# Strassen's scheme on three of eight pairs of k tiles in six groups of columns

## The chip, the cores and the metric

One Trainium2 chip, one of its cores. A kernel is one program that runs on five engines: TensorE (PE: matmuls; PEld: its weight loads), VectorE (DVE), ScalarE (ACT), GpSimd (POOL) and SyncE (SP, which here only issues DMA transfers). Each engine works through its own instructions in order and waits on semaphores for the others. The metric is the device time of one execution in microseconds; the kernel before takes 978.75 us in the median of three runs (978.57 to 978.86).

## The reference

One residual layer on x of 256 tokens by 2048 channels, float32. All large work is products of these 256 rows with weights, each 2048 deep:

```
h    = rmsnorm(x) ;  proj = h @ w_in          # 2048 x 16400: q k v o z | gates | u z | g_a g_b
h_t  = mlstm(q, k, v, i, f)                   # 8 heads of 256
y_a  = sigmoid(o) * norm(h_t) * silu(z_a)     # 2048 wide
y_b  = (multiscale_pool(u) @ pool_w) * silu(z_b)   # 1024 wide
merged = sigmoid(g_a) * (y_a @ w_proj_mlstm) + sigmoid(g_b) * (y_b @ w_proj_pool)
out    = x + rmsnorm(merged @ w_out)
```

## The kernel before, in words

**Precision.** Every float32 product is made of three matmuls of type float32r: each operand is split into a high part (a cast) and a low part (the operand less its high part), and high·high, low·high and high·low are added in PSUM. `hi_lo` does the split: the cast on ScalarE (line 62), the subtraction on VectorE (line 63).

**Stages.** (1) The input projection for the pooling branch and the mLSTM, with the statistics of the norm, the mLSTM gates, convolutions, pooling and the mLSTM itself run as side work in between. (2) For each of four blocks j of 512 columns: the two gates g_a and g_b (`xtiles(12 + j)` and `xtiles(16 + j)`, 16 k tiles each), the pooling projection (8 k tiles of `wpp`), the mLSTM projection (16 k tiles of `wpm`), then the merge, which is transposed to `m_h`, `m_l`. (3) The output projection in four blocks of 512 columns; the last is ordered so that the rows end one half after the other.

**A token block.** `tok_block` (line 112) makes 512 columns for both halves t of the tokens, in two PSUM banks of the pool `acc` (4 banks; a second pool, `sm`, has the other 4). It goes through the weights in tiles of 128 x 2048 (1 MB). SP loads a tile into `raw` (3 buffers). Each half of a tile, here called a **piece**, is split into `wh`, `wl` (128 x 1024 each, 4 buffers of each) and then used for 12 matmuls of 128x512: 8 with `wh` (high and low part of the activations), 4 with `wl`. A `raw` buffer is free for the next load when VectorE has made the low part of its second piece; a buffer of `wh` or `wl` is free when TensorE is through with the piece four before.

**Order.** The engines' orders come from a scheduler of the framework, which moves instructions forward where their operands allow. Side work is written as generators: `step()` after each piece lets each advance to its next `yield`. The statistics of the norm are such a generator (`stats`, line 231): four squares on ScalarE, a power on GpSimd that gives `rstd`, then `stats_bc` (line 256), which scales the identity by `rstd` on VectorE (`dg`, line 261) and spreads it over partitions by two small matmuls (line 262) into `rstd_bc`. The gates' matmuls (line 286) and ScalarE's sigmoid with `rstd` (line 573) belong to the same time.

Of the kernel before, what the change touches and what calls it, by code (L numbers as in the profile page):

```python
# [17 lines left out]
P = 128  # L18
D = 2048
# [7 lines left out]
WARM = 9  # L27
QD = 32
XW = T + 512
EPS = 1e-6  # L30
# [9 lines left out]
def block_kernel(ctx: ExitStack, tc: tile.TileContext, a: dict, out: bass.AP):  # L40
# [44 lines left out]

    xs_ctx = ExitStack()
    xp = xs_ctx.enter_context(tc.tile_pool(name="xp", bufs=1))
    xc = xp.tile([P, KT, 2, T], F32R, name="xc")
    ybp = xs_ctx.enter_context(tc.tile_pool(name="ybp", bufs=1))
    yb_h = ybp.tile([P, KT // 2, T], F32R, name="yb_h")  # L90
# [19 lines left out]

    def tok_block(tiles, st_h, st_l, load=w_tile):

        ps = [acc.tile([P, 512], F32, name="acc") for _ in range(2)]
        n = 4 * len(tiles)
# [117 lines left out]
    def stats():  # L232
# [17 lines left out]
        rsqrt_mean(rstd, ms, D)  # L250
        for _ in range(3):
            yield 1
        stats_bc()
        ready.append(1)

    def stats_bc():

        pb = small()
        for t in range(2):
            dg = sp.tile([P, P], F32, name="dg", bufs=2)  # L260
            nc.vector.tensor_scalar(dg, ident, rstd[:, t : t + 1], None, op0=ALU.mult)
            nc.tensor.matmul(pb[:, t * P : (t + 1) * P], ones_f, dg, start=True, stop=True)
        nc.vector.tensor_copy(rstd_bc, pb[:, :T])
# [177 lines left out]

    yp = xs_ctx.enter_context(tc.tile_pool(name="yp", bufs=1))
    y_h = yp.tile([P, KT, T], F32R, name="y_h")
# [155 lines left out]
    def st(tile_):  # L599
        return lambda k, t: tile_[:, k, t * P : (t + 1) * P]  # L600

    def merge(j, t, m):
        pt = small()
# [5 lines left out]
    def merges(j, ms):  # L609
        for t in range(2):  # L610
            yield 1
            merge(j, t, ms[t])

    for j in range(4):
        gs = []
        for n in range(2):
            pg = tok_block(xtiles(12 + 4 * n + j), xh, xl)
            for t in range(2):
                s = gate.tile([P, 512], F32, name="g", tag=f"g{t}")
                nc.scalar.activation(s, pg[t], AF.Sigmoid, scale=rstd[:, t : t + 1])  # L620
                gs.append(s)
        drain()
        if j == 0:
            ph1_ctx.close()
            late = ctx.enter_context(tc.tile_pool(name="late", bufs=1, side="right"))
            m_h = late.tile([P, KT, T], F32R, name="m_h")
            m_l = late.tile([P, KT, T], F32R, name="m_l")
        pb = tok_block(
            [a["wpp"][j, i].rearrange("p k c -> p (k c)") for i in range(2)], st(yb_h), st(yb_l)
        )  # L630
        for t in range(2):
            nc.vector.tensor_tensor(gs[2 + t], pb[t], gs[2 + t], op=ALU.mult)
        pa = tok_block(
            [a["wpm"][j, i].rearrange("p k c -> p (k c)") for i in range(4)], st(y_h), st(y_l)
        )
        for t in range(2):
            m = gs[t]
            nc.vector.tensor_tensor(m, pa[t], m, op=ALU.mult)
            nc.vector.tensor_tensor(m, m, gs[2 + t], op=ALU.add)
        side.append(merges(j, gs[:2]))  # L640
    xs_ctx.close()


    osplit = ctx.enter_context(tc.tile_pool(name="osplit", bufs=4, side="right"))
    fin = ctx.enter_context(tc.tile_pool(name="fin", bufs=1))
    post = fin.tile([P, D], F32, name="post")
    nc.scalar.dma_start(post, a["post"])
    xr = [fin.tile([P, D], F32, name=f"xr{t}") for t in range(2)]
    for t in range(2):
        nc.scalar.dma_start(xr[t], a["x"][t * P : (t + 1) * P, :])  # L650
    ob = [fin.tile([P, D], F32, name=f"ob{t}") for t in range(2)]
    s4 = fin.tile([P, 2, 5], F32, name="s4")
# [30 lines left out]

    def otiles(j):
        return [a["wo"][j, i].rearrange("p k c -> p (k c)") for i in range(4)]

    for j in range(3):
        po = tok_block(otiles(j), st(m_h), st(m_l), lambda src: w_tile(src, osplit))
        for t in range(2):
            sums(t, j, j * 512, (j + 1) * 512, po[t])  # L690
            weigh(t, j * 512, (j + 1) * 512, po[t])

    m_hi, m_lo = st(m_h), st(m_l)
    ws = []
    for half in range(8):
        if half % 2 == 0:
            raw = rawp.tile([P, 2048], F32, name="raw")
            nc.sync.dma_start(raw, otiles(3)[half // 2])
        pool, bufs = (fin, 4) if half < 4 else (osplit, None)
        wh = pool.tile([P, 1024], F32R, name="wh", bufs=bufs)  # L700
# [3 lines left out]
    for t, parts in ((0, 1), (1, 2)):  # L704
        for part in range(parts):
            n = 512 // parts
            po = acc.tile([P, 512], F32, name="acc")[:, :n]
            for k in range(KT):
# [17 lines left out]
def _tiles(w, cols, kk):  # L726

    k, n = w.shape
    r = w.reshape(k // (P * kk), kk, P, n // cols, cols)
    return np.ascontiguousarray(r.transpose(3, 0, 2, 1, 4))  # L730


# [57 lines left out]
```

## Time and profile before

| | |
|---|---|
| median of three runs | 978.75 us |
| the profiled execution | 978.46 us |
| its span | 976.7 us (so 1.8 us lie around it) |
| busy in the span: PE, PEld, DVE, ACT, POOL | 99%, 84%, 65%, 51%, 1% |
| TensorE clock granted | 0.998 of full |
| DMA | 187.74 MB, 192 GB/s in the mean |

The first gates' sigmoids start at 596 us, the first squares of the output at 903 us. Matmuls are pipelined and their ends are modelled: each is shown as 0.39 us long, though a next one starts every 0.23 us. So how much TensorE does is read from starts, and whether it waits from the list of waits.

### The profile page before, as it was taken

The page shows a single profiled execution, that of the slowest core. Times are in us where ns is not written, and L with a number is a line of the kernel's source. Part 1 is how long each engine was busy: PE and PEld are TensorE (multiplying, and loading weights), DVE is VectorE, ACT ScalarE, POOL GpSimd, SP SyncE. Part 2 cuts the span into 40 slices and gives each one's busy share as a digit, 9 for nine tenths or more (in the row PEclk, how much of TensorE's full clock was granted, in tenths as well). Part 3 has the DMA queues.
Part 4 walks back from the last instruction along what each step waited for, and adds up shares of the span by engine and source line. Part 5 has one row for each costly group of instructions (what it writes and reads, how often), then busy time and mean ns, then how long its engine had stood idle before and what let it go on. Part 6 is the DMA issues. An engine that isn't in the chain of part 4 may idle for free.

```text
span 976.7 us, 12410 instructions
## 1 busy us (share of the span) xinstructions
PE 965.9 (99%) x4785; PEld 816.4 (84%) x4785; DVE 630.6 (65%) x938; ACT 495.1 (51%) x678; POOL 14.5 (1%) x35
## 2 busy tenths in 40 slices
PE   9999999999999999999999999999999999999996
PEld 6888888888888888888888888888888888888886
DVE  7699776677766867758677686554454455455563
ACT  7756444456644665546554475444444434443451
POOL 1000000000000000000000000000000000000001
PEclk9999999999999999999999999999999999999999
DMA  9755445544455435564555544555555555567542
GB/s 355 296 187 209 173 173 177 211 172 172 157 197 207 173 134 211 172 216 136 191 191 192 196 172 168 179 207 179 178 195 193 210 172 199 189 248 268 180 167 86
DMA packets 29306, 187.74 MB, mean 192 GB/s; under 512 B 3264, under 2 KB 3648, under 8 KB 8256
## 3 DMA queue, kind: packets, MB, share of 16 engines
q1 hardware_dynamic: 28816, 183.81, 52.6%
q10 hardware_dynamic: 432, 3.15, 0.8%
q8 instruction: 37, 0.61, 0.2%
q14 instruction: 21, 0.17, 0.0%
HBM read 184.85 MB, written 2.10 MB: 191 GB/s over the span
## 4 chain that ended last, share of the span: by engine, by line
PE 60%; issue 38%; ACT 1%; POOL 0%; DMA 0%; DVE 0%; DVEq 0%; SPq 0%; POOLq 0%
PE acc L143 18%; PE acc L123 10%; PE acc L124 10%; PE acc L126 10%; PE acc L145 9%; PE sm L72 1%; PE sm L71 1%; PE sm L73 1%; ACT xw L245 0%; PE sm L286 0%; DMA xw<-in_xw 0%; PE sm L559 0%; DVE xr L677 0%; PE sm L508 0%; POOL xr L675 0%
## 5 line engine op out<-in xcount | busy, mean ns | idle before, releaser
L63 DVE TENSOR_TENSOR wl<-raw,wh 128x1024 fp32r<-128x1024 f32 x328 | 398.5, 1223 | 263.6 <-ACT wh L62 263.4
L62 ACT CAST wh<-raw 128x1024 fp32r<-128x1024 f32 x328 | 342.3, 1050 | 370.4 <-PE acc L124 251.9
L123 PE MATMUL acc<-wh,xc 128*128 128x512 f32 x640 | 251.2, 392 | 0.1
L124 PE MATMUL acc<-wh,xc 128*128 128x512 f32 x640 | 249.6, 390 | 0.0
L143 PE MATMUL acc<-xc,wh 128*128 128x512 f32 x768 | 192.5, 392 | 0.0
L126 PE MATMUL acc<-wl,xc 128*128 128x512 f32 x640 | 172.5, 389 | 0.0
L143 PEld LDWEIGHTS acc<-xc,wh 128*128 128x128 f32 x768 | 138.9, 189 | 25.6
L126 PEld LDWEIGHTS acc<-wl,xc 128*128 128x128 f32 x640 | 120.2, 188 | 25.2
L123 PEld LDWEIGHTS acc<-wh,xc 128*128 128x128 f32 x640 | 120.4, 188 | 24.7 <-ACT wh L62 1.0
L124 PEld LDWEIGHTS acc<-wh,xc 128*128 128x128 f32 x640 | 120.4, 188 | 23.9
L145 PEld LDWEIGHTS acc<-xc,wl 128*128 128x128 f32 x768 | 104.8, 190 | 7.5
L145 PE MATMUL acc<-xc,wl 128*128 128x256 f32 x768 | 107.1, 282 | 0.0
L123 PE MATMUL acc<-wh,y_h 128*128 128x512 f32 x128 | 49.8, 389 | 0.0
L124 PE MATMUL acc<-wh,y_l 128*128 128x512 f32 x128 | 49.8, 389 | 0.0
L473 DVE SCALAR_TENSOR_TENSOR cy<-pad,vec,cy 128x256 f32<-128x256 f32 x96 | 39.3, 477 | 0.0
L123 PE MATMUL acc<-wh,m_h 128*128 128x512 f32 x96 | 37.6, 391 | 0.0
L124 PE MATMUL acc<-wh,m_l 128*128 128x512 f32 x96 | 37.4, 389 | 0.0
L126 PE MATMUL acc<-wl,y_h 128*128 128x512 f32 x128 | 34.2, 389 | 0.0
L123 PEld LDWEIGHTS acc<-wh,y_h 128*128 128x128 f32 x128 | 24.0, 188 | 5.0
L124 PEld LDWEIGHTS acc<-wh,y_l 128*128 128x128 f32 x128 | 24.0, 188 | 5.0
L126 PEld LDWEIGHTS acc<-wl,y_h 128*128 128x128 f32 x128 | 24.0, 188 | 5.0
L126 PE MATMUL acc<-wl,m_h 128*128 128x512 f32 x96 | 25.7, 389 | 0.0
(197 smaller groups left out, 771.6 us busy)
## 6 DMA issues: line engine op xcount, KB each, us to landing
raw<-in_wx SPq DMA_DIRECT2D x76, 1024.0 KB, 4.7
raw<-in_wq SPq DMA_DIRECT2D x44, 1024.0 KB, 4.8
raw<-in_wpm SPq DMA_DIRECT2D x16, 1024.0 KB, 4.7
raw<-in_wo SPq DMA_DIRECT2D x16, 1024.0 KB, 4.9
raw<-in_wpp SPq DMA_DIRECT2D x8, 1024.0 KB, 4.7
xw<-in_xw SPq DMA_DIRECT2D x15, 384.0 KB, 6.0
raw<-in_wq SPq DMA_DIRECT2D x8, 512.0 KB, 8.1
xw<-in_x SPq DMA_DIRECT2D x4, 512.0 KB, 8.3
```

Of the source, the lines that this page charges most:

```text
L62: nc.scalar.copy(hi, src)
L63: nc.vector.tensor_tensor(lo, src, hi.bitcast(F32), op=ALU.subtract)
L71: nc.tensor.matmul(ps, lh, rh, start=start, stop=False)
L72: nc.tensor.matmul(ps, ll, rh, start=False, stop=False)
L73: nc.tensor.matmul(ps, lh, rl, start=False, stop=stop)
L123: nc.tensor.matmul(ps[t], st_h(k, t), wh[:, cols], start=k == 0, stop=False)
L124: nc.tensor.matmul(ps[t], st_l(k, t), wh[:, cols], start=False, stop=False)
L126: nc.tensor.matmul(ps[t], st_h(k, t), wl[:, cols], start=False, stop=k == n - 1)
L143: nc.tensor.matmul(ps[c], wh[:, cols], xc[:, k], start=k == 0, stop=False)
L145: nc.tensor.matmul(ps[c][:, 1], wl[:, cols], xc[:, k, 0], start=False, stop=k == KT - 1)
L473: nc.vector.scalar_tensor_tensor(y, pad[:, 1 + j : 1 + j + T], cw[:, j : j + 1], y, op0=ALU.mult, op1=ALU.add)
```

## The change

Six groups of 1024 columns are taken out of the token blocks: three of gates (g_b of blocks 0 and 1, g_a of 2 and 3, g_b of 2 and 3), two of the mLSTM projection, one of the output (columns 0 to 1023). A group has four results C (t, c), one for each half of the tokens and each half of the columns, in four banks. Its 16 k tiles are eight pairs (k, k + 8), and a load of 1 MB (`ws`) brings one pair for both halves of the columns. Five pairs go as before: two pieces of 12 matmuls. Three pairs (`NS`, numbers 0 to 2) go by Strassen's scheme in Winograd's form: seven products of blocks in place of eight, 21 matmuls in place of 24. The order of the pairs in a group is 3, 4, 0, 5, 1, 6, 2, 7.

- For the weights of such a pair VectorE makes four sums of blocks (`t13`, 128x1024; `t24`, two of 128x512), and the pair is split in four pieces of 512, 1024, 1024 and 1024 columns, with 3, 6, 6 and 6 matmuls.
- For the activations four sums are made once for each of x, y and m (`s_forms`), which takes two of the three `raw` buffers while it lasts.
- Four products add into four banks of the other PSUM pool, the rest straight into C; after the third pair these four are combined (`e11` to `e22`: two copies on ScalarE, four sums on VectorE), and added to C at the group's end.
- All gates come ahead of the projections now, and their results are kept; m takes the place of x in `xc`; output block 2 comes first, then the group of blocks 0 and 1, then block 3.
- In `stats` two `yield`s fewer come before `stats_bc`, and the first of its two matmuls is kept in program order.

```diff
@@ stats, stats_bc @@
         rsqrt_mean(rstd, ms, D)
-        for _ in range(3):
-            yield 1
+        yield 1
         stats_bc()
...
-            nc.tensor.matmul(pb[:, t * P : (t + 1) * P], ones_f, dg, start=True, stop=True)
+            i = nc.tensor.matmul(pb[:, t * P : (t + 1) * P], ones_f, dg, start=True, stop=True)
+            if t == 0:
+                tc.keep_in_program_order(i)
@@ new functions @@
+    def s_forms(hl):
+        f = rawp.tile([P, 2048], F32, name="raw")[:, : 2 * NS * T].rearrange("p (h k t) -> p h k t", h=2, k=NS)
+        for h in range(2):
+            nc.vector.tensor_tensor(f[:, h], hl(0, h).bitcast(F32), hl(1, h).bitcast(F32), op=ALU.add)
+        (a11, a21), (a12, a22) = ([f[:, h, :, t * P : (t + 1) * P] for t in range(2)] for h in range(2))
+        r = rawp.tile([P, 2048], F32, name="raw")[:, : 4 * NS * P].rearrange("p (s k t) -> p s k t", s=4, k=NS)
+        nc.vector.tensor_tensor(r[:, 0], a21, a22, op=ALU.add)
+        nc.vector.tensor_tensor(r[:, 1], r[:, 0], a11, op=ALU.subtract)
+        nc.vector.tensor_tensor(r[:, 2], a11, a21, op=ALU.subtract)
+        nc.vector.tensor_tensor(r[:, 3], a12, r[:, 1], op=ALU.subtract)
...
+        hi_lo(s_h, s_l, r)
+        return s_h, s_l
+
+    def group(gi, st_h, st_l, forms, get_a, get_b):
+        s_h, s_l = forms
+        C = {(t, c): get_a() for t in range(2) for c in range(2)}
...
+        for kp in order:
+            raw = rawp.tile([P, 2048], F32, name="raw")
+            nc.sync.dma_start(raw, a["ws"][gi, kp])
+            b4 = raw.rearrange("p (b n) -> p b n", b=4)
+            if kp >= NS:
+                for h in range(2):
...
+                    hi_lo(wh, wl, raw[:, h * 1024 : (h + 1) * 1024])
...
+                continue
...
+            nc.vector.tensor_tensor(t13, b4[:, 1:4:2], b4[:, 0:2], op=ALU.subtract)
+            nc.vector.tensor_tensor(t24[:, 0], b4[:, 3], t13[:, 0], op=ALU.subtract)
+            nc.vector.tensor_tensor(t24[:, 1], b4[:, 2], t24[:, 0], op=ALU.subtract)
...
+            for src, n, jobs in (
+                (raw[:, 0:512], 512, ((0, ps[0], x_(0, 0), last),)),
+                (raw[:, 1024:2048], 1024, (((0, 0), C[0, 0], x_(1, 0), False), ((0, 1), C[0, 1], form(3), False))),
+                (flat[0], 1024, ((1, ps[1], form(0), last), (3, ps[3], form(2), last))),
+                (flat[1], 1024, ((2, ps[2], form(1), last), ((1, 0), C[1, 0], x_(1, 1), False))),
+            ):
...
+                hi_lo(wh[:, :n], wl[:, :n], src)
...
+            if last:
...
+                nc.scalar.copy(e11, ps[0])
+                nc.scalar.copy(e22, ps[1])
+                nc.vector.tensor_tensor(e21, ps[2], e11, op=ALU.add)
+                nc.vector.tensor_tensor(e12, e21, e22, op=ALU.add)
+                nc.vector.tensor_tensor(e21, ps[3], e21, op=ALU.add)
+                nc.vector.tensor_tensor(e22, e21, e22, op=ALU.add)
+        return C, {(0, 0): e11, (0, 1): e12, (1, 0): e21, (1, 1): e22}
@@ gates, projections, output @@
-    for j in range(4):
-        gs = []
-        for n in range(2):
-            pg = tok_block(xtiles(12 + 4 * n + j), xh, xl)
...
+    for j in range(2):
+        pg = tok_block(xtiles(12 + j), xh, xl)
...
+    forms = s_forms(lambda part, h: xc[:, 8 * h : 8 * h + NS, part])
+    for gi, (n, j0) in enumerate(((1, 0), (0, 2), (1, 2))):
+        C, E = group(gi, xh, xl, forms, *((bank, small) if gi % 2 == 0 else (small, bank)))
+        for (t, c), ps in C.items():
+            g_ = lateg.tile([P, 512], F32, name=f"g{n}{j0 + c}{t}")
+            nc.vector.tensor_tensor(g_, ps, E[t, c], op=ALU.add)
+            nc.scalar.activation(g_, g_, AF.Sigmoid, scale=rstd[:, t : t + 1])
...
+    forms = s_forms(lambda part, h: (y_h, y_l)[part][:, 8 * h : 8 * h + NS])
...
+        C, E = group(3 + jp, st(y_h), st(y_l), forms, bank, small)
...
+    po2 = tok_block(otiles(2), st(m_h), st(m_l), get=small)
+    drain()
+    forms = s_forms(lambda part, h: (m_h, m_l)[part][:, 8 * h : 8 * h + NS])
...
+    C, E = group(5, st(m_h), st(m_l), forms, bank, small)
```

The scheduler's order shows the places at which instructions move. First TensorE in the statistics, behind the second piece of the first channel block. `acc_370`, `acc_371` are that block's banks, `wh_440` its third piece; `dg` carries `rstd`, `gc` are the gates' weights. Before:

```order
L145 MATMUL acc_370<-xc_76,wl_414 128x256
L145 MATMUL acc_371<-xc_76,wl_414 128x256
L262 MATMUL sm_589<-dg_590,ones_f_109 128x128
L262 MATMUL sm_589<-dg_593,ones_f_109 128x128
L286 MATMUL sm_663<-xc_76,gc0_405 128x512 x4
L286 MATMUL sm_663<-xc_76,gc1_407 128x512
L143 MATMUL acc_370<-xc_76,wh_440 128x512
L143 MATMUL acc_371<-xc_76,wh_440 128x512
```

With the change (lines of the new kernel) the third piece follows at once,

```order
L149 MATMUL acc_370<-xc_76,wl_414 128x256
L149 MATMUL acc_371<-xc_76,wl_414 128x256
L147 MATMUL acc_370<-xc_76,wh_440 128x512
L147 MATMUL acc_371<-xc_76,wh_440 128x512
L147 MATMUL acc_370<-xc_76,wh_440 128x512
```

and four pieces later (`wh_559` is the second block's third piece):

```order
L149 MATMUL acc_493<-xc_76,wl_523 128x256
L265 MATMUL sm_542<-dg_543,ones_f_109 128x128
L265 MATMUL sm_542<-dg_546,ones_f_109 128x128
L147 MATMUL acc_492<-xc_76,wh_559 128x512
L147 MATMUL acc_493<-xc_76,wh_559 128x512
```

The two matmuls with `dg` have moved back by four pieces, and the five of the gates that stood with them to where the other eleven are.

Second, VectorE around the first group. Before, it splits piece after piece, with the low parts of y in between (`wl_5555` is the last piece of the second gate block, `wl_5585` the first of the next block):

```order
L63 TENSOR_TENSOR wl_5487<-raw_5468,wh_5486 128x1024
L63 TENSOR_TENSOR wl_5505<-raw_5502,wh_5504 128x1024
L66 SCALAR_TENSOR_TENSOR y_l_1366<-sm_5434,vec_82,y_h_1365 128x256
L63 TENSOR_TENSOR wl_5521<-raw_5502,wh_5520 128x1024
L66 SCALAR_TENSOR_TENSOR y_l_1366<-sm_5434,vec_82,y_h_1365 128x256
L66 SCALAR_TENSOR_TENSOR y_l_1366<-sm_5459,vec_82,y_h_1365 128x256
L63 TENSOR_TENSOR wl_5539<-raw_5536,wh_5538 128x1024
L66 SCALAR_TENSOR_TENSOR y_l_1366<-sm_5459,vec_82,y_h_1365 128x256
L63 TENSOR_TENSOR wl_5555<-raw_5536,wh_5554 128x1024
L63 TENSOR_TENSOR wl_5585<-raw_5582,wh_5584 128x1024
```

With the change the six instructions of the forms (lines 612 to 618) stand between `wl_5487` and `wl_5555`, and in the group itself, from the first Strassen pair (`raw_5665`) over an ordinary one (`raw_5713`) to the second Strassen pair (`raw_5747`), VectorE has:

```order
L64 TENSOR_TENSOR wl_5684<-raw_5665,wh_5683 128x1024
L673 TENSOR_TENSOR t13_5749<-raw_5747 128x1024
L674 TENSOR_TENSOR t24_5750<-raw_5747,t13_5749 128x512
L64 TENSOR_TENSOR wl_5694<-t13_5671,wh_5693 128x1024
L675 TENSOR_TENSOR t24_5750<-raw_5747,t24_5750 128x512
L64 TENSOR_TENSOR wl_5704<-t24_5672,wh_5703 128x1024
L64 TENSOR_TENSOR wl_5716<-raw_5713,wh_5715 128x1024
L64 TENSOR_TENSOR wl_5732<-raw_5713,wh_5731 128x1024
L64 TENSOR_TENSOR wl_5755<-raw_5747,wh_5754 128x512
L64 TENSOR_TENSOR wl_5762<-raw_5747,wh_5761 128x1024
L64 TENSOR_TENSOR wl_5772<-t13_5749,wh_5771 128x1024
L673 TENSOR_TENSOR t13_5827<-raw_5825 128x1024
```

The sums of the second Strassen pair stand ahead of the last two pieces of the first one; those of the third (`t13_5827`) behind the second's third piece.

Third, VectorE at the end of the third gate group, where the forms of y (`raw_6589`, `raw_6592`) are made; `wl_6514`, `wl_6524` are the last two pieces of its last Strassen pair, `raw_6543` is its last pair, `wl_6607` the first piece of the pooling projection:

```order
L612 TENSOR_TENSOR raw_6589<-y_h_1365,y_l_1366 128x768
L64 TENSOR_TENSOR wl_6514<-t13_6491,wh_6513 128x1024
L615 TENSOR_TENSOR raw_6592<-raw_6589 128x384
L617 TENSOR_TENSOR raw_6592<-raw_6589 128x384
L616 TENSOR_TENSOR raw_6592<-raw_6592,raw_6589 128x384
L64 TENSOR_TENSOR wl_6524<-t24_6492,wh_6523 128x1024
L64 TENSOR_TENSOR wl_6546<-raw_6543,wh_6545 128x1024
L618 TENSOR_TENSOR raw_6592<-raw_6589,raw_6592 128x384
L64 TENSOR_TENSOR wl_6562<-raw_6543,wh_6561 128x1024
L698 TENSOR_TENSOR e2_6535<-sm_6333,e0_6533 128x512
```

Since the forms hold two `raw` buffers, the pooling projection's first load takes that of `raw_6543`, which `wl_6562` frees.

More of the change, by code (lines that the diff above doesn't have):

```diff
@@ L109, in w_tile, with bank, tok_block @@
             yield c0, c1, wh, wl
-    def tok_block(tiles, st_h, st_l, load=w_tile):
-        ps = [acc.tile([P, 512], F32, name="acc") for _ in range(2)]
+    def bank():
+        return acc.tile([P, 512], F32, name="acc")
+    def tok_block(tiles, st_h, st_l, load=w_tile, get=bank):
+        ps = [get() for _ in range(2)]
         n = 4 * len(tiles)
@@ L602, in merge @@
     def merge(j, t, m):
-        pt = small()
+        pt = bank()
         for c in range(4):
@@ L620, in block_kernel @@
-                nc.scalar.activation(s, pg[t], AF.Sigmoid, scale=rstd[:, t : t + 1])
-                gs.append(s)
+                nc.vector.tensor_tensor(gs[1, j, t], pb[t], gs[1, j, t], op=ALU.mult)
         drain()
[L623 to L630, printed above, removed]
```

136 lines of the change are left out of this document (103 added, 33 removed).

## The prediction

> **What bounds the kernel now.** The page's busy shares, then TensorE's list of waits, then rows by stage:
>
> ```profile
> PE 965.9 (99%) x4785; PEld 816.4 (84%) x4785; DVE 630.6 (65%) x938; ACT 495.1 (51%) x678; POOL 14.5 (1%) x35
> PE sm L262 <- DVE dg L261: 1.6, 1, 1.6
> PE sm L166 <- DVE zeros L161: 1.2, 1, 1.2
> 700.00:750.00 50.00, 50.00 (x226) 41.38 (x225) 26.81 (x27) 21.24 (x22) 0.00 (x0) 1.00 0.53 190
> ```
>
> A PE busy share of 99% alone would prove little, since matmuls are shown longer than their spacing. The waits do: in the whole span TensorE waits for another engine twice, both at the start. In the stage of gates and projections (the last row: stretch, sum, PE, PEld, DVE, ACT, POOL, clock, DMA share, GB/s) VectorE has 26.8 of 50 us, ScalarE 21.2, DMA half its time. So a matmul taken out there counts in full, until another engine becomes late. What one costs is read from VectorE's beat in a token block, where each low part waits for a buffer that TensorE gives back:
>
> ```profile
> 908.45 1.22 DVE L63 TENSOR_TENSOR wl<-raw,wh 128x1024 fp32r<-128x1024 f32 x1 [1.50 <-ACT wh L62]
> 911.17 1.23 DVE L63 TENSOR_TENSOR wl<-raw,wh 128x1024 fp32r<-128x1024 f32 x1 [1.50 <-ACT wh L62]
> 913.89 1.23 DVE L63 TENSOR_TENSOR wl<-raw,wh 128x1024 fp32r<-128x1024 f32 x1 [1.50 <-ACT wh L62]
> ```
>
> One piece, 12 matmuls, every 2.72 us: 0.227 us a matmul.
>
> **The change part by part. Matmuls.** Each group drops 3 of 24 in three pairs: 6 x 3 x 3 = 54, so 54 x 0.227 = **-12.2 us**. The 1 MB loads stay as many. A group lasts (5 x 24 + 3 x 21) x 0.227 = 41.5 us on TensorE; a Strassen pair 4.8 us, an ordinary one 5.4.
>
> **VectorE in a group.** Its prices:
>
> ```profile
> L63 DVE TENSOR_TENSOR wl<-raw,wh 128x1024 fp32r<-128x1024 f32 x328 | 398.5, 1223 | 263.6 <-ACT wh L62 263.4
> L639 DVE TENSOR_TENSOR g<-g 128x512 f32<-128x512 f32 x8 | 5.1, 682 | 0.0
> L632 DVE TENSOR_TENSOR g<-acc,g 128x512 f32<-128x512 f32 x8 | 5.2, 686 | 4.4 <-PE acc L126 4.4
> 931.85 3.50 DVE L63 TENSOR_TENSOR wl<-raw,wh 128x1024 fp32r<-128x1024 f32 x3 [0.42 <-ACT wh L62]
> 904.15 1.28 DVE L660 TENSOR_TENSOR ob<-acc,post 128x512 f32<-128x512 f32 x2
> ```
>
> Three in a row take 3.50 us where one takes 1.22, so they start (3.50 - 1.22) / 2 = 1.14 us apart; two of 512 take 1.28, 0.60 apart, or 0.72 where one needs the other's result (0.68 and a hand-over of 0.04). Between the two sizes lie 1.05 ns an element; by that line 768 elements take 0.95 us (0.87 apart), 384 take 0.55, 1536 take 1.76: estimates. A group has 19 low parts of 1024 (21.7 us), 3 of 512 (1.8), 3 `t13` (3.4), 6 halves of `t24` (4.0), 4 sums of e (2.6) and 4 additions to C (2.4): 35.9 of 41.5 us, 87%, in place of 16 low parts, 18.2. In the stretch of one Strassen and one ordinary pair it is 9.2 (6.9 without the lead that the two next sums may take, and 2.3) of 10.2. It is not the bound, but near it, and it keeps TensorE covered only while it is some pieces ahead. Four buffers of `wl` let it be three pieces ahead, 8 us in ordinary pieces, 4 in Strassen's. ScalarE has 10 casts of 1.05, three of 0.61, nine more of 1.05, two copies and four sigmoids, about 26 us: covered.
>
> **Entry to the first group.** The last gate block before, with the times of its last pieces (VectorE's order is in the section on the change):
>
> ```profile
> 596.13 1.21 DVE L63 TENSOR_TENSOR wl<-raw,wh 128x1024 fp32r<-128x1024 f32 x1
> 602.06 0.19 PEld L123 LDWEIGHTS acc<-wh,xc 128*128 128x128 f32 x1
> 604.35 1.05 ACT L62 CAST wh<-raw 128x1024 fp32r<-128x1024 f32 x1 [1.31 <-PE acc L124]
> 605.44 1.23 DVE L63 TENSOR_TENSOR wl<-raw,wh 128x1024 fp32r<-128x1024 f32 x1 [1.11 <-ACT wh L62]
> 606.70 16.59 SPq L104 DMA_DIRECT2D raw<-in_wpm  x4
> raw<-in_wx SPq DMA_DIRECT2D x76, 1024.0 KB, 4.7
> GB/s 0 0 0 0 0 170 210 380 433 393 92 66 144 301 419 433 315 26 0 0 105 262 433 419 419 39 0 0 52 170 223 406 446 380 0 0 0 210 39 393
> L620 ACT ACTIVATE g<-acc,rstd 128x512 f32<-128x512 f32 x16 | 10.1, 684 | 0.0
> ```
>
> The cast at 604.35 is that of the block's last piece, and waited for the piece four before, which TensorE began at 602.06; so the block ends at 602.06 + 5 x 2.72 = 615.7. The forms put 2 x 0.87 and about 2.2 us of sums ahead of the low part at 605.44; idle time takes up part, and it ends at 607.4, not 606.7. Then the freed buffer is loaded, landing 4.7 us later at 612.2; the next load, issued with it, 2.4 us behind (1 MB at 433 GB/s, the highest of 40 slices around it) at 614.6. Four casts, the last after 614.6 + 1.05 + 0.95 = 616.6, stand ahead of the two sigmoids that empty the banks of the block, and the group's third and fourth bank are those two. TensorE asks for the third at 615.7 + 4 x 0.227 = 616.6 and gets it at 617.3: **+0.7 us** (nothing if the second load lands 0.7 us sooner; 1.6 with VectorE 1 us later).
>
> **Forms of y.** The pooling projection's first load waits for `wl_6562`. From there: landing 4.7, cast 1.05, hand-overs 0.2: 6.0 us. `wl_6562` cannot be made before TensorE is through with the piece four before; then TensorE still has 1.36 + 1.36 + 2.72 + 2.72 = 8.2 us and VectorE's 1.2 go off, 6.9 left: no wait. If VectorE is late by all it does for the forms up to there (1.7 + 2.2 = 4.0 us), 2.9 are left: 3.1 us of wait. From `wl_6497` on VectorE has 10.0 us for these six pieces with the forms, TensorE 10.2: it neither gains nor loses, and I take it 1.9 us behind its best: **+1.0**. The forms of m follow ordinary pieces, with 10.9 us in place of 8.2 behind the freeing low part: nothing.
>
> **Loads within a group.** The second and third Strassen pair's loads wait for the second low part of an ordinary pair; between that and their first sum VectorE has 4.2 and 2.9 us of work, the landing takes 4.7. So VectorE idles 0.5 and 1.8, 2.3 us a group: 35.9 + 2.3 = 38.2 is still below 41.5, and its lead hides it. With the merges' additions and the last block's start I allow **+1.2** in all, between nothing and 6 x 2.3 = 13.8.
>
> **Statistics.** TensorE, ScalarE:
>
> ```profile
> 32.10 1.11 PE L145 MATMUL acc<-xc,wl 128*128 128x256 f32 x8
> 34.84 0.71 PE L262 MATMUL sm<-dg,ones_f 128*128 128x128 f32 x4 [1.63 <-DVE dg L261]
> 35.31 1.41 PE L286 MATMUL sm<-xc,gc 128*128 128x512 f32 x5
> 36.55 2.00 PE L143 MATMUL acc<-xc,wh 128*128 128x512 f32 x8
> 34.50 0.72 ACT L573 ACTIVATE g<-g,rstd 128x512 f32<-128x512 f32 x1 [1.21 <-POOL rstd L193]
> 35.13 1.04 ACT L62 CAST wh<-raw 128x1024 fp32r<-128x1024 f32 x1
> ```
>
> The wait for `dg` goes, but the piece that comes up in its place has its cast at 35.13, behind a sigmoid that waits for the same `rstd`. TensorE then waits until 36.2: the piece starts 0.3 us earlier than at 36.55, and the 1.7 us of work from 34.84 to 36.55 that filled this time is done later. Less about 0.2 for two matmuls without a wait: **+1.2 us**. What is late next is `rstd_bc`, at 47.7 in place of 35.6; the side work behind it feeds no piece.
>
> The sum: -12.2 + 0.7 + 1.0 + 1.2 + 1.2 = -8.1 against the profiled execution's 978.46 gives 970.4; the median shown is 0.3 higher, so I say **970.5 us**.
>
> [...] By row 931.85 an instruction of VectorE starts 0.09 us before the one ahead ends. [...]
>
> **The rivals.** (1) *VectorE's lead covers everything*: only matmuls and statistics count, 978.46 - 12.2 + 1.2 + 0.3 = 967.7. For it: 87%. Against: the two entries above are worked out from landings, not shares. Chance 0.12.
>
> (2) *VectorE loses its lead at every form and seam*: each of three forms costs the 3.1 us of the worst case, the entry 1.6, and half of the load waits, 6.9, go through: -12.2 + 1.2 + 1.6 + 9.3 + 6.9 = +6.8 at the worst, 985.5; with half of these stalls -12.2 + 1.2 + 8.9 = -2.1, 976.6. I put it at 975 to 978. For it: a VectorE a few per cent slower than its rows (strided operands, which no row shows) would do it. Against: the sizes are those of rows. Chance 0.14.
>
> (3) *VectorE's instructions take their full length each*: 42 of them a group in the mean, 0.085 more each, 3.6 us; with forms 3.0 us a group, 35.9 + 3.6 + 3.0 = 42.5 against 41.5. It is the bound: six times 1.0 us. An engine that is behind anyway cannot lose a lead again, so I count the three forms' 3.1 and the entry's 1.6 by half, 5.5: -12.2 + 1.2 + 6.0 + 5.5 = +0.5, 979.3, no change. Chance 0.04.
>
> (4) *Slower: the loads of the Strassen pairs.* The 2.3 us that VectorE idles for two loads in each group reach TensorE, since the sums stand ahead of the last pieces of the pair before: 6 x 2.3 = 13.8 more in place of 1.2, 978.46 - 12.2 + 1.2 + 0.7 + 1.0 + 13.8 + 0.3 = 983.3. It decides where VectorE stands less than 2.3 us ahead of TensorE when it comes to `t13`. For it: three `raw` buffers and the order of the sums. Against: its lead of three pieces. Chance 0.09.
>
> That fewer matmuls are dropped than said is excluded by the order's count.
>
> **How the numbers follow.** 0.2%, 2 us, is about what a measurement of this kernel can tell from no change, so faster ends at 976.8 and slower begins at 980.7. Forecast 0.61 (967 to 974), the rivals as given: faster is 0.61 + 0.12 + two thirds of (2) = 0.82; same 0.05 of (2) and 0.04 of (3), 0.09; slower 0.09. The range goes from 966.5, 1.2 below rival (1), to the end of (2), 977.5; outside lie (3), (4) and a little.
>
> **What would show it.** TensorE's wait for `dg` gone and one of 3 us for a cast at 33 to 36 us in its place; one of under 1.6 us for a sigmoid at the first group's third bank; one of 0 to 3 us for a cast at the pooling projection's first piece; VectorE some 87% busy in the groups, with waits for `raw` ahead of `t13`. Wrong would be: repeated waits of TensorE for low parts inside groups (2, 4), or a beat of VectorE of 1.22 us in a row of three (3).

## The result and the profile after

The changed kernel takes 971.25 us in the median of four runs (970.8 to 971.56), the kernel before beside it 978.66 us. The ratio is 0.9924 with a 95% interval of 0.9911 to 0.9936: 7.4 us faster. The forecast was 970.5 us, with a range of 966.5 to 977.5.

The profiled execution took 971.45 us, with a span of 969.6. From its page, the busy shares:

```profile
PE 956.9 (99%) x4731; PEld 807.4 (83%) x4731; DVE 746.3 (77%) x1097; ACT 535.5 (55%) x730; POOL 14.5 (1%) x35
```

TensorE's list of waits in the whole span (us in total, times, the longest):

```profile
PE acc L147 <- ACT wh L63: 3.0, 1, 3.0
...
PE acc L641 <- ACT g L721: 0.6, 1, 0.6
```

TensorE has 54 matmuls fewer (4785 to 4731), VectorE 116 us more work. Two waits are new, both announced: 3.0 us for a cast, and 0.6 us for a sigmoid at the first group's third bank. None stands in the groups, and none at the pooling projection. The span fell by 976.7 - 969.6 = 7.1 us, 5.1 less than the 12.2 of the matmuls alone. Where these 5.1 us are is read at three places.

**The statistics.** TensorE's timeline from the second piece of the first channel block on (start, duration, engine, line):

```profile
31.96 1.11 PE L149 MATMUL acc<-xc,wl 128*128 128x256 f32 x8
36.07 3.69 PE L147 MATMUL acc<-xc,wh 128*128 128x512 f32 x8 [3.00 <-ACT wh L63]
40.55 2.00 PE L147 MATMUL acc<-xc,wh 128*128 128x512 f32 x8
```

The same time in stretches of 1 us; the third number from the end is the granted clock:

```profile
36.00:37.00 1.00, 0.93 (x2) 0.81 (x3) 0.95 (x1) 1.00 (x3) 0.00 (x0) 0.56 0.04 16
37.00:38.00 1.00, 1.00 (x4) 0.75 (x3) 0.67 (x2) 1.00 (x2) 0.00 (x0) 0.50 0.00 0
38.00:39.00 1.00, 1.00 (x4) 0.81 (x3) 1.00 (x2) 1.00 (x2) 0.00 (x0) 0.50 0.00 0
39.00:40.00 1.00, 1.00 (x6) 0.85 (x6) 1.00 (x2) 0.68 (x2) 0.00 (x0) 0.73 0.54 66
```

The piece that comes up in place of the `dg` matmuls waits until 36.07, as forecast (36.2). But then its eight matmuls show 3.69 us where before, at 36.55, they showed 2.00: the granted clock is 0.50. The rows add up to 0.88 + 1 + 1 + 0.54 = 3.4 us at half clock. The piece after it, in the timeline of before:

```profile
39.34 2.00 PE L143 MATMUL acc<-xc,wh 128*128 128x512 f32 x8
```

Now it starts 40.55 - 31.96 = 8.59 us behind the second one; before, it was 39.34 - 32.10 = 7.24, and 1.7 us of that was other work, which is now done later (some 0.2 us shorter, without its wait). So 1.35 + 1.7 - 0.2 = 2.85 us, in place of the 1.2 forecast.

**The entry to the first group.** TensorE there:

```profile
619.39 0.39 PE L643 MATMUL acc<-wh,xc 128*128 128x512 f32 x1
620.35 0.50 PE L641 MATMUL acc<-wh,xc 128*128 128x512 f32 x1 [0.57 <-ACT g L721]
```

The first row is the fourth matmul, the last on the first two banks; then comes the third bank. It would have started at 619.39 + 0.23 = 619.62 and starts at 620.35, 0.73 later; the matmul behind it loses another 0.1.

**Inside the groups.** The stretch of the three gate groups (stretch, sum, PE, PEld, DVE, ACT), and that of the first group of the mLSTM projection:

```profile
618.71:744.92 126.21, 125.64 (x551) 102.99 (x550) 110.15 (x119) 74.12 (x83) 0.00 (x0) 1.00 0.52 191
766.68:808.46 41.78, 41.78 (x185) 34.36 (x184) 33.66 (x35) 22.63 (x25) 0.00 (x0) 1.00 0.55 194
```

TensorE in a Strassen pair (six matmuls from the first row to the last), and in an ordinary pair (four):

```profile
653.12 0.40 PE L641 MATMUL sm<-wh,s_h 128*128 128x512 f32 x1
...
654.52 0.40 PE L641 MATMUL sm<-wh,s_h 128*128 128x512 f32 x1
...
656.60 0.39 PE L643 MATMUL acc<-wh,xc 128*128 128x512 f32 x1
...
657.50 0.39 PE L643 MATMUL acc<-wh,xc 128*128 128x512 f32 x1
```

VectorE is busy 110.15 of 126.21 us, 87%, as worked out. A group without a stall lasts 41.78 us where 183 matmuls at 0.2267 make 41.48. The 0.3 us are no wait: in the Strassen pair the starts lie (654.52 - 653.12) / 6 = 0.233 us apart, in the ordinary one (657.50 - 656.60) / 4 = 0.225. Six groups make 1.8 us.

So -12.2 + 2.85 + 0.83 + 1.8 = -6.7, which leaves 0.4 of the measured -7.1 to small differences elsewhere.

### The profile page after: what moved, and what is told of

It is laid out like the page before. It is cut to its first block, busy times and chain, and to the rows that moved or that the text cites. A ratio compares the mean times of both kernels' runs of the same rounds, so it can differ in the third digit from the quotient of the medians.

```text
span 969.6 us, 12590 instructions
## 1 busy us (share of the span) xinstructions
PE 956.9 (99%) x4731; PEld 807.4 (83%) x4731; DVE 746.3 (77%) x1097; ACT 535.5 (55%) x730; POOL 14.5 (1%) x35
## 4 chain that ended last, share of the span: by engine, by line
PE 61%; issue 37%; ACT 1%; POOL 0%; DVE 0%; DVEq 0%; ACTq 0%; POOLq 0%
PE acc L147 18%; PE acc L127 10%; PE acc L128 10%; PE acc L130 10%; PE acc L149 9%; PE sm L72 1%; PE sm L73 1%; PE sm L74 1%; PE sm L170 0%; PE sm L291 0%; ACT xw L249 0%; PE sm L564 0%; DVE xr L799 0%; PE sm L513 0%; POOL xr L797 0%
## 5 line engine op out<-in xcount | busy, mean ns | idle before, releaser
L64 DVE TENSOR_TENSOR wl<-raw,wh 128x1024 fp32r<-128x1024 f32 (+1 forms) x328 | 387.0, 1191 | 140.6 <-ACT wh L63 138.5
L63 ACT CAST wh<-raw 128x1024 fp32r<-128x1024 f32 (+1 forms) x328 | 334.7, 1028 | 281.8 <-PE acc L147 96.0
L127 PE MATMUL acc<-wh,xc 128*128 128x512 f32 x448 | 175.8, 392 | 0.0
L128 PE MATMUL acc<-wh,xc 128*128 128x512 f32 x448 | 174.7, 390 | 0.0
L130 PE MATMUL acc<-wl,xc 128*128 128x512 f32 x448 | 121.2, 389 | 0.0
L130 PEld LDWEIGHTS acc<-wl,xc 128*128 128x128 f32 x448 | 84.1, 188 | 17.7
L127 PEld LDWEIGHTS acc<-wh,xc 128*128 128x128 f32 x448 | 84.2, 188 | 17.5 <-ACT wh L63 1.2
L128 PEld LDWEIGHTS acc<-wh,xc 128*128 128x128 f32 x448 | 84.2, 188 | 16.5
L63 ACT CAST wh<-t 128x1024 fp32r<-128x1024 f32 x36 | 37.9, 1052 | 53.5 <-PE acc L643 41.4
L64 DVE TENSOR_TENSOR wl<-t,wh 128x1024 fp32r<-128x1024 f32 x36 | 44.0, 1223 | 20.1 <-ACT wh L63 20.1
L641 PE MATMUL acc<-wh,xc 128*128 128x512 f32 x141 | 55.0, 390 | 0.6 <-ACT g L721 0.6
L643 PE MATMUL acc<-wh,xc 128*128 128x512 f32 x141 | 55.0, 390 | 0.0
L645 PE MATMUL acc<-wl,xc 128*128 128x512 f32 x141 | 40.5, 390 | 0.0
L643 PE MATMUL acc<-wh,y_l 128*128 128x512 f32 x92 | 35.9, 390 | 0.0
L641 PE MATMUL acc<-wh,y_h 128*128 128x512 f32 x92 | 35.8, 390 | 0.0
L641 PEld LDWEIGHTS acc<-wh,xc 128*128 128x128 f32 x141 | 26.5, 188 | 6.6 <-ACT g L721 1.0
L645 PEld LDWEIGHTS acc<-wl,xc 128*128 128x128 f32 x141 | 26.5, 188 | 5.6
```

Source lines behind the costliest of these rows:

```text
L63: nc.scalar.copy(hi, src)
L64: nc.vector.tensor_tensor(lo, src, hi.bitcast(F32), op=ALU.subtract)
L127: nc.tensor.matmul(ps[t], st_h(k, t), wh[:, cols], start=k == 0, stop=False)
L128: nc.tensor.matmul(ps[t], st_l(k, t), wh[:, cols], start=False, stop=False)
L130: nc.tensor.matmul(ps[t], st_h(k, t), wl[:, cols], start=False, stop=k == n - 1)
L641: nc.tensor.matmul(dst, lh, wh, start=key not in begun, stop=False)
```

## The experiments

The theories at the start: **A**, the costs lie where the changed trace shows them, 2.8 us in the statistics (half of it clock), 0.8 at the third bank, and a Strassen pair is worth its matmuls. **B**, the prediction's own sizes, 1.2 us for the statistics. Behind them stood the question how far VectorE was from being the bound.

### The statistics as before

```diff
-        yield 1
+        for _ in range(3):
+            yield 1
         stats_bc()
...
-            i = nc.tensor.matmul(pb[:, t * P : (t + 1) * P], ones_f, dg, start=True, stop=True)
-            if t == 0:
-                tc.keep_in_program_order(i)
+            nc.tensor.matmul(pb[:, t * P : (t + 1) * P], ones_f, dg, start=True, stop=True)
```

> The changed kernel with the statistics as before (three yields, the matmul with dg free to move). Theory A, read from the changed trace: the move costs 2.8 us, 1.4 more of idle time at 33 to 36 us and 1.4 of matmuls at half clock behind it, so this kernel takes 968.4 us against 971.25, shows no granted clock under 1.00 between 30 and 50 us, and its only early waits of TensorE are the one for dg (1.6 us) and the one for zeros. Theory B, the prediction's term: the move costs 1.2 us, so 970.0.

Measured: 968.29 us (967.96 to 968.73), ratio 0.9892 (0.9877 to 0.9907). It is 3.0 us less than the change, theory A's number. TensorE's list:

```profile
PE sm L266 <- DVE dg L265: 1.6, 1, 1.6
...
```

The short wait for `dg` is back, and the clock stays at 1.00.

### The kernel before with the new statistics

The same lines the other way, in the kernel before.

> The kernel before with nothing but the new statistics. Theory A: 2.8 us slower than before, 981.4, with a 3.0 us wait for a cast at 33 to 36 us and a half clock for 3.4 us behind it. Theory B: 1.2 us slower, 979.9. If the cost belonged to the groups (the later rstd_bc meeting something in them), there would be no loss here at all.

Measured: 981.47 us, ratio 1.0029 (1.0019 to 1.0040), 2.7 us slower: theory A again, and the groups have no part in it. Its seven runs tell more than the median: one took 980.51 with a mean granted clock of 0.998, five 981.3 to 981.7 with 0.996, one 982.96 with 0.995. The median of the kernel before beside it is 978.77, with the same 0.998. So without a half clock the move seems to cost 1.7 us, as far as one execution can tell, and the rest comes in steps. The profiled one waits 3.0 us for the cast as the change does, and the stretch behind the wait has a clock of 0.57:

```profile
36.00:40.00 4.00, 3.72 (x10) 3.01 (x11) 3.41 (x3) 3.71 (x6) 0.00 (x0) 0.57 0.01 2
```

### Filling the idle time

```diff
+                if first_ch and c0:
+                    first_ch.clear()
+                    pw = small()
+                    for _ in range(10):
+                        i = nc.tensor.matmul(pw, zeros[:, 0:P], zeros, start=True, stop=True)
+                        tc.keep_in_program_order(i)
                 step()
```

> The changed kernel with ten matmuls on zeros (128x512 bf16, results unused) behind the second piece of the first channel block, where TensorE idles 3.0 us; they last about 2.3 us and end before the cast that it waits for. Theory A says that the clock drops because of the idle time: the wait stays, the half clock goes, and the kernel takes about 1.4 us less, 969.8. Theory B, only the wait counts: no change, 971.2. If the ten come in the way of the piece behind them, it is slower than 971.3.

Measured: 969.89 us (969.25 to 970.36), ratio 0.9909 (0.9895 to 0.9922): 1.4 us less than the change, by ten matmuls that compute nothing. TensorE's timeline there (nine of the ten are in the trace), and the clock of the stretch behind:

```profile
33.43 2.10 PE L156 MATMUL sm<-zeros 128*128 128x512 bf16 x9
36.36 1.43 PE L147 MATMUL acc<-xc,wh 128*128 128x512 f32 x5 [0.82 <-ACT wh L63]
```

```profile
36.00:40.00 4.00, 3.64 (x20) 3.18 (x21) 3.32 (x3) 4.00 (x6) 0.00 (x0) 1.00 0.00 1
```

The piece still waits for its cast (36.36), but the idle time is 0.82 us and the clock behind it 1.00. So of the 3.0 us that the statistics cost, 1.4 were the clock by the medians, and 1.6 (969.89 - 968.29) the wait and the work put off. The timelines put a little more on the clock: the piece that started 8.59 us behind the second one in the change starts 7.01 us behind it here, 1.6 us sooner, and 1.3 us are left for the rest.

### Other banks for the first group

```diff
     drain()
+    bank, small = small, bank
     ph1_ctx.close()
```

> The changed kernel with the two PSUM pools exchanged from the first group on, so that its four results start in banks that no gate block holds. By the trace TensorE's stall at the third bank is 0.85 us (0.73 and 0.11 by the starts), so 970.4. Rival: the bank was not the only thing late; then a wait for a cast or a low part comes up at the same place and the time stays within 0.3 us of 971.25.

Measured: 971.40 us (970.77 to 971.83), ratio 0.9924 (0.9912 to 0.9937). The wait for the sigmoid is gone from the list, nothing stands in its place, and the profiled span is 968.9 us, 0.7 less; the median is not lower. Part of that may be the clock: the two longest of the five runs (971.77 and 971.83) have a mean granted clock of 0.995, the four of the change 0.996 or 0.997. With the old statistics as well:

> The changed kernel with the old statistics and the exchanged PSUM pools. If the two add: 968.3 less the 0.7 us of the stall at the third bank that the trace of the exchanged pools no longer shows, 967.6. If the stall's end gains nothing, as that run's time of 971.4 says: 968.3.

Measured: 968.05 us (967.74 to 968.13), ratio 0.9894 (0.9879 to 0.9909), 0.24 less than with the old statistics alone, but the kernel before beside it took 0.22 less too (978.55 for 978.77). The stall is what the trace says, a bank that waits for its sigmoid; what it is worth over many runs, between nothing and 0.7 us, these runs cannot tell.

### Two pairs, four pairs, and one more sum

```diff
-NS = 3
+NS = 2
```

> The changed kernel with two pairs in place of three by Strassen's scheme (NS = 2): 18 matmuls more, so 18 x 0.227 = 4.1 us, less a third of the 1.4 us by which matmuls in the groups' Strassen pairs stand further apart than elsewhere: 971.25 + 4.1 - 0.5 = 974.9. Rival: a Strassen pair has a cost that the list of waits doesn't show, so that the third brings less than it drops; then under 974.3.

Measured: 974.62 us, ratio 0.9964 (0.9952 to 0.9977). The third pair is worth 3.4 us by the medians, 2.8 by the profiled executions (974.27 and 971.45), where 18 matmuls make 4.1. The wider spacing takes a part: the first group of the mLSTM projection lasts 42.36 us here, where 186 matmuls make 42.17; with three pairs it was 41.78 for 41.48. That is 0.58 us less a group, 3.5 in six. The wait for the sigmoid at the third bank, 0.8 us with three pairs, is not in TensorE's list with two.

```profile
767.77:810.13 42.36, 42.36 (x188) 34.92 (x186) 29.89 (x31) 20.94 (x23) 0.00 (x0) 1.00 0.56 198
```

Then four pairs:

```diff
-NS = 3
+NS = 4
...
-        rest = list(range(NS, 8))
...
-        order += rest[2 + NS :]
+        order = [4, 0, 5, 1, 6, 2, 3, 7]
```

> The changed kernel with four pairs by Strassen's scheme (NS = 4, pairs in the order 4, 0, 5, 1, 6, 2, 3, 7): 18 matmuls fewer, a group of 40.8 us on TensorE. VectorE gets one low part of 1024, one of 512, one t13 and one t24 more, 1.14 + 0.60 + 1.14 + 1.35 = 4.2 us, so 40.1 in a gate group, with the larger forms over 41. Theory A: VectorE is now the bound, TensorE's list shows repeated waits for low parts in the groups, and of the 4.1 us nothing is left or more than that is lost: 971 to 976. Theory B: the lead hides it: 967.6. Theory C, the prediction's slower rival, the loads' waits come on top of it in each group: 985.

Measured: 978.69 us (977.83 to 980.94), ratio 1.0003 (0.9994 to 1.0012). The fourth pair gives back everything, 7.4 us more than three pairs. That is more than theory A allowed (971 to 976), and the place is not the one it named: TensorE's list has no wait for a low part in the groups. The longest in the list:

```profile
PE sm L127 <- ACT wh L63: 5.3, 1, 5.3
PE acc L147 <- ACT wh L63: 3.0, 1, 3.0
PE acc L636 <- ACT wh L63: 2.1, 1, 2.1
...
```

The timeline of VectorE, ScalarE and TensorE at the end of the third gate group, where the pooling projection begins:

```profile
744.55 0.69 DVE L618 TENSOR_TENSOR raw<-raw 128x512 f32<-128x512 f32 x1
...
745.33 1.90 ACT L63 CAST s_h<-raw 128x2048 fp32r<-128x2048 f32 x1 [6.37 <-DVE raw L618]
747.13 2.56 ACT L728 ACTIVATE g<-g,rstd 128x512 f32<-128x512 f32 x4
749.59 3.88 ACT L63 CAST wh<-raw 128x1024 fp32r<-128x1024 f32 x4
...
750.67 0.80 PE L127 MATMUL sm<-wh,yb_h 128*128 128x512 f32 x1 [5.28 <-ACT wh L63]
```

The forms of y are done late on VectorE (744.55). On ScalarE their cast stands ahead of the pooling projection's first cast, and idles 6.37 us for them with that cast and four sigmoids queued behind it. The first matmul behind the wait is shown 0.80 us long, twice the 0.39 of one ahead of it (744.10), as at half clock. VectorE has no room in the 50 us up to there:

```profile
700.00:749.80 49.80, 45.40 (x199) 36.93 (x197) 49.45 (x57) 29.26 (x34) 0.00 (x0) 1.00 0.47 166
```

It is busy 49.45 of 49.80 us. So with the forms of y in it, this stretch is full, while the gate groups in the mean are not (96%, shown below). That speaks for the place of the forms at the seam, and the order of the queues behind them, as the cause rather than VectorE's work in the groups as a whole; the runs further below try it.

Then three pairs with one sum made twice:

```diff
             nc.vector.tensor_tensor(t13, b4[:, 1:4:2], b4[:, 0:2], op=ALU.subtract)
+            nc.vector.tensor_tensor(t13, b4[:, 1:4:2], b4[:, 0:2], op=ALU.subtract)
```

> The changed kernel with t13 made twice over in each Strassen pair (the same values), 3 x 1.14 = 3.4 us more of VectorE in each group, 39.3 of 41.5 in a gate group; the same matmuls. If VectorE's lead has this room, as its waits for casts in the groups say, 971.3 to 973 (a few us may come up behind the forms, where VectorE is closest). If VectorE is at its limit already, 6 x 3.4 = 20 us more, 991.

Measured: 976.15 us (974.41 to 978.55), ratio 0.9976 (0.9968 to 0.9985). A quarter of the 20 us that a full VectorE would have made of 18 more sums, but 3 us above the other end. The longest of the waits that are new, again at seams:

```profile
PE sm L130 <- DVE wl L64: 2.3, 1, 2.3
...
PE sm L74 <- DVE wl L64: 0.8, 1, 0.8
...
```

VectorE's timeline at the pooling projection:

```profile
744.59 2.48 DVE L733 TENSOR_TENSOR g<-acc,e 128x512 f32<-128x512 f32 x4 [1.10 <-PE acc L645]
746.99 1.75 DVE L64 TENSOR_TENSOR s_l<-raw,s_h 128x1536 fp32r<-128x1536 f32 x1
748.66 3.49 DVE L64 TENSOR_TENSOR wl<-raw,wh 128x1024 fp32r<-128x1024 f32 x3
```

And the clock behind the wait:

```profile
751.00:755.00 4.00, 4.00 (x12) 3.15 (x11) 2.46 (x4) 1.25 (x2) 0.00 (x0) 0.57 1.01 406
```

VectorE even idles 1.10 us there: its next instruction adds the group's last results and waits for TensorE, and the pooling projection's first low part stands behind that and behind the forms' low part. A wait of 2.3 us follows, and then, by the clock of 0.57 in 4 us, 3.4 us at half clock, an estimated 1.7 us lost: with the 0.8 in the last block 4.8 us, as much as the medians lose (4.9; the profiled execution, at 977.44, lost 6.0).

### Moving the forms

If the seam is the cause, the forms must only stand elsewhere. First with the doubled sums, the forms of y behind the first block of the pooling projection:

```diff
-    forms = s_forms(lambda part, h: (y_h, y_l)[part][:, 8 * h : 8 * h + NS])
...
                 nc.vector.tensor_tensor(gs[1, j, t], pb[t], gs[1, j, t], op=ALU.mult)
+            if j == 0:
+                forms = s_forms(lambda part, h: (y_h, y_l)[part][:, 8 * h : 8 * h + NS])
```

> The kernel with t13 made twice over (976.15 us), and the forms of y made behind the first block of the pooling projection (j = 0) in place of ahead of it. Theory A: of the 4.9 us that the doubled sums cost, the part that TensorE waits at the pooling projection's first piece (2.3 and 0.2 us in that profile) and the half clock of 3.4 us that follows it (1.7 us) come from the forms standing ahead of those pieces on VectorE; they go, and the time is 972. Theory B: VectorE is simply full; the wait moves to another place, and the time stays at 975 to 977.

Measured: 971.66 us (969.84 to 972.73), ratio 0.9921 (0.9907 to 0.9934). That is 0.4 us above the change, so the 18 extra sums are free but for some tenths, if moving the forms alone gains nothing there, which was not run. In the pooling projection TensorE's list has one wait of 0.5 us left, behind the forms' new place. Theory B falls. Then the same with four pairs, the old statistics and the other banks:

> Four pairs, with the old statistics, the exchanged PSUM pools, and the forms of y behind the first block of the pooling projection. From 968.05: 18 matmuls fewer -4.1, their wider spacing +0.5, the waits that four pairs showed at the output's group +2.9 (2.1 and 0.7): 967.4 if the forms of y were the cause of the 5.3 us wait and the half clock at the pooling projection. If VectorE (40.1 of 40.8 us in a gate group) is the bound, the wait comes up elsewhere: 970 or more.

Measured: 971.00 us (969.02 to 971.89), ratio 0.9916 (0.9903 to 0.9929). That is 7.7 us less than 978.69, of which 3.2 are what the old statistics and the other banks bring with three pairs (971.25 - 968.05). But it is 3.6 us above what was expected, and in the range that was said for a VectorE that is the bound. What TensorE still waits for at the seams, and the clock behind the first of these waits:

```profile
PE sm L635 <- ACT wh L63: 2.1, 1, 2.1
...
PE acc L130 <- DVE wl L64: 1.6, 1, 1.6
...
```

```profile
896.00:900.00 4.00, 3.40 (x8) 2.72 (x9) 4.00 (x5) 2.96 (x4) 0.00 (x0) 0.58 0.82 268
```

Two things remained: the forms now stand ahead of the second block's low parts (1.6 us), and the wait of 2.1 us at the output's group, which the expectation had counted, is followed here by the half clock, which it had not counted; with four pairs before, the same wait was not followed by it. So, still with the old statistics and the other banks, the forms went inside the group that uses them, ahead of its first Strassen pair, behind one ordinary pair or two:

```diff
-    forms = s_forms(lambda part, h: xc[:, 8 * h : 8 * h + NS, part])
+    forms = [lambda part, h: xc[:, 8 * h : 8 * h + NS, part]]
...
         for kp in order:
+            if kp == 0 and len(forms) == 1:
+                forms.append(s_forms(forms[0]))
             raw = rawp.tile([P, 2048], F32, name="raw")
```

(y and m in the same way; in the second kernel the order in these groups is 4, 5, 0, 1, 6, 2, 3, 7.)

> Four pairs with the old statistics and the exchanged pools, the forms made inside the group that uses them, just ahead of its first Strassen pair's load (behind one ordinary pair, order 4, 0, 5, 1, 6, 2, 3, 7). Theory A: it is the place of the forms that makes TensorE wait (2.8 us in the pooling projection, 3.9 at the output's group with its half clock, in the run before this one), so up to 6.7 us come back: 964.3. Theory B: VectorE, 40.1 us of work in 40.8 and the forms on top, is full; the wait moves into the groups' second pieces and the time stays at 968 or more.

> The same, with two ordinary pairs ahead of the forms in the groups that make them (order 4, 5, 0, 1, 6, 2, 3, 7 there). TensorE has 10.9 us of ordinary pieces behind which VectorE makes the forms, in place of 5.4, so by theory A at least as fast as the run beside it, 964 to 966; then three Strassen pairs follow with one ordinary pair among them, 6.5 us of VectorE each against 4.8 of TensorE. By theory B slower than the run beside it or the same, 968 or more.

Measured: with one ordinary pair ahead 965.93 us (965.76 to 966.41), ratio 0.9871 (0.9856 to 0.9886), the fastest of all kernels here, 12.7 us below the kernel before and 5.3 below the change. Three pairs with the same statistics and banks took 968.05, so 2.1 of these 5.3 us are the fourth pair with its forms inside. With two ahead 970.36 us (969.02 to 970.49), ratio 0.9911 (0.9894 to 0.9927). What is new in the first one's list, and the stretch of its gate groups:

```profile
PE acc L634 <- ACT wh L63: 1.0, 1, 1.0
```

```profile
615.97:739.57 123.60, 123.60 (x542) 101.38 (x541) 118.53 (x129) 80.23 (x90) 0.00 (x0) 1.00 0.61 215
```

The first kernel with four pairs in most of its gate groups:

```profile
620.00:742.00 122.00, 121.30 (x530) 99.13 (x529) 117.22 (x128) 76.74 (x86) 0.00 (x0) 1.00 0.54 189
```

The longest in the list of the one with two ordinary pairs ahead:

```profile
PE acc L74 <- DVE wl L64: 2.0, 1, 2.0
...
```

VectorE is busy 118.53 of 123.60 us, 96%, in the gate groups, and TensorE waits for nothing there nor at the pooling projection; only at the output's group 1.0 us is left. In the first kernel with four pairs VectorE had the same share (117.22 of 122.00), and TensorE waited 5.3 us behind these groups. There the forms of y fell into the last of the three; now only those of x are made in these groups. So it was the place of the forms, as theory A has it; 1.6 us of what it promised did not come (965.9 for 964.3), 1.0 of them this wait. With two ordinary pairs ahead, the Strassen pairs crowd at the group's end. In the output's group, and in no other, TensorE waits for low parts, 0.9 us in three places, and in the last block behind it 2.0 us, followed by the half clock (from 940.58 to 942.71 six starts lie 0.43 us apart, from 943.99 on 0.23; 1.7 us lost is an estimate, from 3.4 us of it as in the change). That makes 4.6 us, about the 4.4 by which this kernel is slower. In that group theory B held.

## Why the prediction was right, point by point

The time was 0.75 us above the forecast, and the terms show that part of this was luck: the statistics cost 1.8 us more than said and the matmuls of the Strassen pairs 1.8 that no term had, against 1.0 and 1.2 us for stalls that did not come.

- **The matmuls, -12.2.** Right. Groups with two, three and four pairs confirm the price, less 0.1 us for each Strassen pair, a spacing that no row of before showed.
- **The statistics, +1.2: the term that was mis-sized.** It measured 3.0. The sequence was right: the wait for `dg` gone, a wait of 3 us for the cast, the piece at 36.07 (36.2 said). The part without the clock was 1.6 by the medians, 1.3 by the timelines, rather than 1.2. What the step put at nothing is the half clock behind a wait of 3.0 us, 1.4 us by the medians and 1.6 by the timelines. The rows of before could not show it: their longest wait is 1.6 us, and the clock behind it 1.00 (34 to 40 us).
- **The entry, +0.7.** Right in place, cause and size (0.73 and 0.1).
- **The forms of y, +1.0.** Nothing was lost. One premise, which the section on the change has too, was wrong: the pooling projection's first load does not wait for `wl_6562`. In the changed kernel the transfer is issued at 738.26, when the last sum of the forms ends (737.64 + 0.55), while `wl_6562` runs until 739.33. The timeline of VectorE, SP's queue, ScalarE and TensorE:

```profile
737.64 0.55 DVE L618 TENSOR_TENSOR raw<-raw 128x384 f32<-128x384 f32 x1
738.11 1.22 DVE L64 TENSOR_TENSOR wl<-raw,wh 128x1024 fp32r<-128x1024 f32 x1
738.26 10.98 SPq L105 DMA_DIRECT2D raw<-in_wpp  x4
743.05 2.01 ACT L63 CAST wh<-raw 128x1024 fp32r<-128x1024 f32 x2 [2.12 <-DMA raw<-in_wpp]
744.92 0.39 PE L127 MATMUL sm<-wh,yb_h 128*128 128x512 f32 x1
```

  The buffer is that of the forms' first sums. The cast ends at 744.10, 0.8 us before TensorE asks.
- **The allowance of 1.2 for loads, merges and seams.** Nothing of that kind was lost; the 1.8 us of wider spacing took its place. Why those matmuls start later was not tried and stays open.
- **Rival (1), the lead covers everything:** true of VectorE in this kernel, but for the entry. Its 967.7 was 3.6 us too low all the same: the statistics (1.8 more), the entry (0.8) and the spacing (1.8) were not in it.
- **Rival (2), lost leads at forms and seams:** not the case with three pairs, but the right place to look. One more sum a pair brought it, at the seams alone, and it went when the forms of y stood elsewhere with the same work on VectorE.
- **Rival (3), full lengths:** false. Two low parts in a row take 2.36 us, not 2.44, in VectorE's timeline of the changed kernel (and three take 3.49 in the one with one more sum, shown above):

```profile
614.89 2.36 DVE L64 TENSOR_TENSOR wl<-raw,wh 128x1024 fp32r<-128x1024 f32 x2 [2.65 <-ACT wh L63]
```

- **Rival (4), the loads of the Strassen pairs:** false. VectorE waits for them in the whole kernel as long as the rival had it in each group (its list of waits), and TensorE never does:

```profile
DVE t L673 <- DMA raw<-in_ws: 2.3, 4, 1.1
```

## What to carry to other kernels

A wait of TensorE, where it bounds the kernel, can cost more than its length (here 3.0 us of it were followed by 3.4 us at half clock, 1.4 us by the medians): look at the granted clock in the stretch behind it, and where a wait of 2 us or more can't be avoided, try some idle matmuls to fill it (done here once, for the wait of 3.0 us). When an added load makes an engine late, ask first where in the order the late instruction stands, and behind which waiting instruction, before calling the engine full: here VectorE carried 96% in the gate groups without a wait of TensorE, once the forms stood elsewhere. It was full only in the 50 us where they had stood, and their place had cost more than the fourth pair brings.

## What the runs showed of the hardware

In these traces the halved clock comes in steps. The same wait of 3.0 us was followed by 3.4 us at half clock in the changed kernel, and with four pairs by twice that, 0.9 + 5 + 0.9 = 6.8 (in stretches):

```profile
36.00:37.00 1.00, 0.24 (x1) 0.24 (x2) 0.26 (x1) 1.00 (x2) 0.00 (x0) 0.54 0.09 37
37.00:42.00 5.00, 5.00 (x16) 4.23 (x17) 4.46 (x4) 4.21 (x5) 0.00 (x0) 0.50 0.27 62
42.00:43.00 1.00, 1.00 (x5) 0.81 (x4) 0.65 (x1) 0.00 (x0) 0.00 (x0) 0.55 1.02 434
```

And a wait of 2.1 us at the output's group was followed by the half clock in one kernel (0.58 from 896 to 900, shown above) and not in another, the first one with four pairs. Its timeline, and the stretch behind:

```profile
906.94 0.50 PE L636 MATMUL acc<-wh,xc 128*128 128x512 f32 x1 [2.06 <-ACT wh L63]
```

```profile
907.00:911.00 4.00, 4.00 (x18) 3.27 (x19) 4.00 (x6) 2.75 (x4) 0.00 (x0) 1.00 0.83 274
```

Nor does the clock fall at a fixed place. With four pairs it falls at 36.08 (0.92 us at half clock between 36 and 37), when TensorE has been idle for 2.3 us, 0.7 us before its next matmul; with the other banks, if it stays at half clock until 40, it falls at 36.96, 0.6 us after the matmuls have begun again. The first matmuls behind the wait with four pairs, then those with the other banks and the stretch there:

```profile
36.76 1.22 PE L147 MATMUL acc<-xc,wh 128*128 128x512 f32 x2 [3.00 <-ACT wh L63]
```

```profile
36.32 1.56 PE L147 MATMUL acc<-xc,wh 128*128 128x512 f32 x4 [3.00 <-ACT wh L63]
36.00:40.00 4.00, 3.68 (x11) 3.02 (x12) 3.37 (x3) 4.00 (x6) 0.00 (x0) 0.62 0.02 6
```

How much idle time brings it is read from these traces alone. 1.6 us was not followed by the half clock in the kernel before and in the change with the old statistics (1.00 in the stretches behind it), 2.0 and 2.3 us were, 2.1 us once and once not, and 3.0 us was in the four profiles whose stretch behind it is given here (the change, before with the new statistics, other banks, four pairs). What decides it at about 2 us is not shown; no run was made to find it. The times spread with the clock: the kernel with one more sum, with its waits of 3.0 and 2.3 us, took 974.41 to 978.55 us at mean clocks of 0.997 to 0.993, the fastest one, with none over 1.6, 965.76 to 966.41 at 0.998 and 0.997.
